# Issuing both steps of every weight split to the scheduler as if 400 instructions sooner

## The chip, the cores and the metric

The kernel runs on one core of one Trainium2 chip. The metric is device time in microseconds (us) of one execution, the median of several. Engines are named as in the profile: PE is TensorE's matmul, PEld its weight load, DVE is VectorE, ACT is ScalarE, POOL is GpSimd, SP is SyncE, which here issues DMAs only.

## The reference

Two blocks follow each other on one sequence of 512 tokens of width 1024; the first also reads 256 context tokens. Everything is float32.

```python
def first_block(x, c, ctx, ...):          # 2 hybrid layers
    ...
def hybrid_layer(xs, cs, c, c_ctx, ..., need_ctx):
    ...
    px = split_cols(hx @ w_in + b_in)     # 1024 -> N_IN
    pc = split_cols(hc @ w_in + b_in)
    ya_x = conv_module(*px[0:3], ...)     # depthwise conv of width 31, layer norm, w_conv_out
    yb_x, yb_c = gla_branch(px[3:9], pc[3:9], ...)    # 4 heads, chunks of 64, two directions
    yc_x, yc_c = attn_branch(px[9:13], pc[9:13], ...) # 8 heads, 2 key heads
    def merge(p, ya, yb, yc):
        return (jax.nn.sigmoid(p[13]) * ya + jax.nn.sigmoid(p[14]) * yb
                + jax.nn.sigmoid(p[15]) * yc) @ w_out
```

The second block has two layers, each with a big input projection, a chunked mLSTM branch and a chunked retention branch of four heads each, and an output projection.

## The kernel before, in words

**Weights.** All big weights are packed on the host into granules of 128 partitions by up to 1024 floats, in the order of use. For each granule `split` does three things: SP loads it into a tile `wr` (`raw`, L270); ACT writes its rounded high part `wh` (a copy, L285); DVE subtracts to get the low part `wl` (L286). `wr`, `wh` and `wl` have two buffers each, so a third split waits until the matmuls that read the first have ended. Some splits of block 2 and of the output projections go to spare columns of the tiles `hh` and `hl` in place of `wh` and `wl`. There are 358 splits. One small weight, that of the GLA's low-rank gate, is split by code of its own (L908, L909).

**Matmuls.** `mm3` (L317) multiplies in three passes: high by high, high by low, low by high. Activations are split into `hh`/`hl` (or `bh`/`bl` for a branch's output) in the same way. The results go to PSUM tiles called `pp`; there are three of them in block 1 and four in block 2. The matmuls that write `pp` are the projections, and PE's bulk of work.

**Order.** The program is written as one instruction sequence and a scheduler deals it out to the engines. Each engine works its list in that order. An instruction's place in the program is its priority; `tc.high_priority(offset=n)` gives the instructions inside it the priority of a place n instructions sooner. The scheduler puts what is ready, by its own reckoning, and first in priority on an engine's list first. In block 1 `_weave` writes a dependent chain (the GLA's heads, the attention's heads) and projection work by turns. `_lifted(..., 200)` already lifts the projection work that is woven into the attention, by 200; that woven into the GLA is not lifted.

**The GLA chain.** For each of four heads: a gate (`z` matmul L948, Exp and Ln on ACT, an add L953, two scans L956 and L958 on DVE, exponentials on ACT, the products `kin` L977 and `bk` L978 on DVE), transposes of `bk` on PE (L984), state products on PE (L998) and a state recurrence `SP` on DVE (L1008), masked scores (L1021, L1025), outputs on PE (L1029, L1033), then the head's norm (per-token sums L625, a reciprocal root on DVE L302 to L308, a transposing matmul L635). `bk` (L935, L936) is copied out of a `pp` tile by ACT beforehand. Last in a layer's first half the attention runs, whose value matmuls are L1264, and its output `ao` is made on DVE (L1272).

The projection work beside the chain ("fill" below) are the L317 matmuls into `pp`, whose results ACT and DVE read out (`merged` L763 and L775, `tf`).

Of the kernel before, what the change touches and what calls it, by code (L numbers as in the profile page):

```python
# [9 lines left out]
F32 = mybir.dt.float32  # L10
# [4 lines left out]
AF = mybir.ActivationFunctionType  # L15
ALU = mybir.AluOpType
# [243 lines left out]
class _K:  # L260
# [12 lines left out]
    def split(self, spec, spare=None):  # L273

        nk, nc_ = spec[3], spec[5]
        n = nk * nc_
        r = self.raw(spec)[:, :n]
        if spare is None:
            hi = self.wh.tile([P, 1024], F32R, tag="wh", name="wh")[:, :n]
            lo = self.wh.tile([P, 1024], F32R, tag="wl", name="wl")[:, :n]  # L280
        else:
            c = slice(TX + P * spare, TX + P * spare + n // KT)
            hi, lo = self.hh[:, :, c], self.hl[:, :, c]
            r = r.rearrange("p (k c) -> p k c", k=KT)
        self.nc.scalar.activation(hi, r, AF.Copy)  # L285
        self.nc.vector.tensor_tensor(out=lo, in0=r, in1=hi.bitcast(F32), op=ALU.subtract)  # L286
        return hi, lo

    @staticmethod
# [1066 lines left out]
def _second_block(K, ctx, res, pend):  # L1356
# [79 lines left out]
    for l in range(DEPTH):  # L1436
# [123 lines left out]
        def mixer(kind, hd):  # L1560
# [4 lines left out]
            if ml:  # L1565
                for which, c0 in enumerate((cq, ck)):
                    for i in range(2):
                        cc = 8 * which + 2 * hd + i
                        ps = tin(c0 + 256 * hd + 128 * i)
                        u = hp.tile([P, 515], F32, name="u", bufs=2)  # L1570
                        G.memset(u[:, 0:3], 0.0)
                        S.activation(u[:, 3:515], ps, AF.Copy)  # L1572
                        ac = tt()
                        V.tensor_scalar(out=ac, in0=u[:, 0:512], scalar1=vec("cw", 4 * cc), scalar2=vec("cb", cc),
                                        op0=ALU.mult, op1=ALU.add)
                        for t in range(1, 4):
                            V.scalar_tensor_tensor(out=ac, in0=u[:, t:t + 512], scalar=vec("cw", 4 * cc + t), in1=ac,
                                                   op0=ALU.mult, op1=ALU.add)
                        th = tt()
                        S.activation(th, ac, AF.Tanh, scale=0.5)  # L1580
                        V.scalar_tensor_tensor(out=ac, in0=th, scalar=1.0, in1=ac, op0=ALU.add, op1=ALU.mult)
                        qk.append(split(ac, 0.5 if which == 0 else 0.5 / 16, f"qk{which}{i}"))
            else:
                for which, c0 in enumerate((cq, ck)):
                    p2 = [tin(c0 + 256 * hd + 128 * i) for i in range(2)]
                    t = [tt(), tt(), tt(), tt()]
                    V.tensor_tensor(out=t[0], in0=p2[0], in1=cos, op=ALU.mult)
                    V.tensor_tensor(out=t[1], in0=p2[0], in1=sin, op=ALU.mult)
                    V.tensor_tensor(out=t[2], in0=p2[1], in1=sin, op=ALU.mult)
                    V.tensor_tensor(out=t[3], in0=p2[1], in1=cos, op=ALU.mult)  # L1590
                    V.tensor_tensor(out=t[0], in0=t[0], in1=t[2], op=ALU.subtract)
                    V.tensor_tensor(out=t[1], in0=t[1], in1=t[3], op=ALU.add)
                    for i in range(2):
                        qk.append(split(t[i], 1.0 if which == 0 else 1.0 / 16, f"qk{which}{i}"))
# [211 lines left out]
```

## Time and profile before

| | before |
|---|---|
| time, median of 3 executions | 2748.11 us (2747.8 to 2751.84) |
| profiled execution | 2749.59 us |
| span of that execution, first to last instruction | 2747.5 us |
| mean granted clock of PE | 0.977 |
| PE busy | 2609.0 us (95%) |
| DVE busy | 1984.6 us (72%) |
| ACT busy | 1089.8 us (40%) |

The span is the time in which instructions ran; some 2 us of the execution lie around it. A granted clock of 1.00 is 2.4 GHz, a stretch with 0.50 would be at 1.2 GHz all through, and a value between is a mixture of the two levels.

### The profile page before, as it was taken

What the parts mean: (1) busy time and instruction counts of PE and PEld (TensorE: products, weight loads), DVE (VectorE), ACT (ScalarE), POOL (GpSimd) and SP (SyncE); (2) the same over time, 40 slices, a digit from 0 to 9 for tenths busy, and PEclk for the clock granted to TensorE, in tenths of its full rate; (3) what the DMA queues carried; (4) which work ended last, traced back from release to release, by engine and by line L of the source; (5) the groups of instructions that cost most, each with busy time, mean ns of one, the idle gap of its engine ahead of it and who ended that gap; (6) DMA issues with size and microseconds to landing.
All of it is one profiled execution on the core that took longest, in us unless ns stands there. A gap on an engine that the chain in (4) does not pass through costs nothing.

```text
span 2747.5 us, 37004 instructions
## 1 busy us (share of the span) xinstructions
PE 2609.0 (95%) x14484; PEld 2222.0 (81%) x14484; DVE 1984.6 (72%) x3691; ACT 1089.8 (40%) x1819; POOL 27.8 (1%) x94
## 2 busy tenths in 40 slices
PE   5998899999899999699999989999999999999998
PEld 3887778888788788578877878888888978888887
DVE  5998565677875599766888678776677678655665
ACT  3234423454532334534545344442333444432332
POOL 0000000000000000000000000000000000000000
PEclk9999999999999999899999999999999999999999
DMA  5210103101253231013134424334332222223222
GB/s 210 64 56 29 39 28 103 55 30 62 71 156 100 88 97 62 27 61 112 58 111 130 139 80 137 121 117 130 123 123 77 82 82 83 84 80 92 77 85 77
DMA packets 78110, 243.18 MB, mean 89 GB/s; under 512 B 9968, under 2 KB 16496, under 8 KB 77808
## 3 DMA queue, kind: packets, MB, share of 16 engines
q1 hardware_dynamic: 72448, 233.37, 27.2%
q10 hardware_dynamic: 5488, 7.44, 0.9%
q8 instruction: 114, 1.87, 0.3%
q14 instruction: 60, 0.49, 0.1%
HBM read 238.68 MB, written 2.10 MB: 88 GB/s over the span
## 4 chain that ended last, share of the span: by engine, by line
PE 79%; DVE 15%; ACT 3%; issue 2%; DMA 1%; ACTq 0%; POOL 0%; DVEq 0%
PE pp L317 63%; PE pm L317 5%; DVE ca L814 4%; PE ov L1264 2%; DVE wl L286 2%; PE sc L1234 2%; DVE SP L1008 2%; PE tr L1254 2%; ACT wh L285 1%; PE pm L1033 1%; PE pm L635 1%; PE pm L625 1%; DVE t L958 1%; PE pm L1685 1%; DVE t L956 0%
## 5 line engine op out<-in xcount | busy, mean ns | idle before, releaser
L317 PE MATMUL pp<-hh,wh 128*128 128x512 f32 (+1 forms) x2080 | 772.5, 373 | 35.1 <-ACT bk L936 12.4
L317 PE MATMUL pp<-hh,wl 128*128 128x512 f32 (+1 forms) x2080 | 768.0, 372 | 28.8 <-DVE wl L286 28.7
L317 PE MATMUL pp<-hl,wh 128*128 128x512 f32 (+1 forms) x2080 | 767.9, 371 | 1.4 <-DVE hl L472 1.3
L285 ACT ACTIVATE wh<-wr 128x1024 fp32r<-128x1024 f32 (+1 forms) x348 | 347.6, 1000 | 769.1 <-PE pp L317 696.8
L286 DVE TENSOR_TENSOR wl<-wr,wh 128x1024 fp32r<-128x1024 f32 (+1 forms) x348 | 399.2, 1148 | 195.5 <-ACT wh L285 190.4
L317 PEld LDWEIGHTS pp<-hh,wh 128*128 128x128 f32 x2080 | 396.6, 191 | 103.2 <-ACT bk L936 13.1
L317 PEld LDWEIGHTS pp<-hh,wl 128*128 128x128 f32 x2080 | 396.4, 191 | 100.7 <-DVE wl L286 36.4
L317 PEld LDWEIGHTS pp<-hl,wh 128*128 128x128 f32 x2080 | 396.9, 191 | 64.8 <-DVE hl L472 3.4
L317 PE MATMUL pp<-wl,hh 128*128 128x256 f32 (+1 forms) x704 | 227.8, 324 | 3.4 <-DVE wl L286 3.2
L317 PE MATMUL pp<-wh,hh 128*128 128x256 f32 (+1 forms) x704 | 225.1, 323 | 3.2 <-ACT u L1572 2.7
L317 PE MATMUL pp<-wh,hl 128*128 128x256 f32 (+1 forms) x704 | 226.3, 322 | 0.0
L814 DVE SCALAR_TENSOR_TENSOR ca<-u,sm,ca 128x783 f32<-128x783 f32 (+1 forms) x240 | 201.7, 890 | 1.1
L317 PEld LDWEIGHTS pp<-wl,hh 128*128 128x128 f32 x704 | 133.8, 190 | 17.0 <-DVE wl L286 7.0
L317 PEld LDWEIGHTS pp<-wh,hh 128*128 128x128 f32 x704 | 133.2, 190 | 15.6 <-ACT u L1572 3.5
L317 PEld LDWEIGHTS pp<-wh,hl 128*128 128x128 f32 x704 | 133.8, 190 | 10.1
L417 DVE CUSTOM_DVE_ANT_0 junk<-mw,cond,bmod 128x1024 bf16<-128x1024 f32 x104 | 132.8, 1277 | 3.4 <-DMA mw<-modw 3.1
L317 PE MATMUL pp<-bh,wh 128*128 128x512 f32 (+1 forms) x288 | 105.6, 368 | 7.2 <-DVE merged L775 3.0
L317 PE MATMUL pp<-bl,wh 128*128 128x512 f32 (+1 forms) x288 | 103.4, 360 | 0.0
L317 PE MATMUL pp<-bh,wl 128*128 128x512 f32 (+1 forms) x288 | 103.2, 361 | 0.0
L317 PE MATMUL pp<-yh,wh 128*128 128x512 f32 (+1 forms) x256 | 93.9, 368 | 0.0
L317 PE MATMUL pp<-yh,wl 128*128 128x512 f32 (+1 forms) x256 | 93.5, 366 | 0.0
L317 PE MATMUL pp<-yl,wh 128*128 128x512 f32 (+1 forms) x256 | 93.4, 366 | 0.0
(377 smaller groups left out, 4266.6 us busy)
## 6 DMA issues: line engine op xcount, KB each, us to landing
wr<-wpack SPq DMA_DIRECT2D x308, 512.0 KB, 3.5
mw<-modw SPq DMA_DIRECT2D x80, 512.0 KB, 3.6
wr<-wpack SPq DMA_DIRECT2D x48, 256.0 KB, 2.7
m<-wpack SPq DMA_DIRECT2D x16, 512.0 KB, 8.2
cond<-cond ACTq DMA_DIRECT2D x5, 512.0 KB, 4.0
res<-xT SPq DMA_DIRECT2D x4, 512.0 KB, 4.9
tf<-xT SPq DMA_DIRECT2D x8, 256.0 KB, 2.6
out<-t SPq DMA_DIRECT2D x16, 128.0 KB, 1.8
```

The costliest lines, as they stand in the source:

```text
L285: self.nc.scalar.activation(hi, r, AF.Copy)
L286: self.nc.vector.tensor_tensor(out=lo, in0=r, in1=hi.bitcast(F32), op=ALU.subtract)
L317: mm(o, lhsT=lhs[a], rhs=r[b], start=first and p == 0, stop=last and p == 2)
L417: pin(V.tensor_tensor_reduce(out=junk, in0=w, in1=self.cond[:, v, :], scale=1.0, scalar=bias[:, j:j + 1], op0=ALU.mult, op1=ALU.add, accum ...
L625: T.matmul(p1[:, i:i + 1], lhsT=x[:, o:o + P], rhs=ones[:, 0:1], start=True, stop=True)
L635: T.matmul(p2[:, o:o + P], lhsT=r[:, i:i + 1].to_broadcast([P, P]), rhs=ident, start=True, stop=True)
L814: V.scalar_tensor_tensor(out=ca[:, c, :], in0=x, scalar=w, in1=ca[:, c, :], op0=ALU.mult, op1=ALU.add)
L958: V.tensor_tensor_scan(out=cum[64:128, ::-1], data0=reset[64:128, ::-1], data1=ls[64:128, ::-1], initial=0.0, op0=ALU.mult, op1=ALU.add)
L1008: V.scalar_tensor_tensor(out=SP[r, n_, :], in0=SP[r, c_, :], scalar=dec[r, c_:c_ + 1], in1=con[c_][r, :], op0=ALU.mult, op1=ALU.add)
L1234: T.matmul(sc[:, s - k0:e - k0], lhsT=qT[:, t * P:t * P + P], rhs=kT[pi][:, s:e], start=pi == 0, stop=pi == 1)
L1254: T.transpose(tr[:, jj * 256 + q * P:jj * 256 + q * P + P], pr[q][:, (j + jj) * P:(j + jj + 1) * P], ident)
L1264: T.matmul(ov, lhsT=vhl[:, kts[j0 + jj], g].rearrange("p a b -> p (a b)"), rhs=x_[:, jj * 256:jj * 256 + 256], start=j0 + jj + pi == 0, st ...
```

## The change

Both instructions of `split` are written inside `high_priority(offset=400)`. The load of `wr` and the matmuls that read `wh` and `wl` are not. Instructions, tiles, sizes and buffers are those of before.

```diff
             c = slice(TX + P * spare, TX + P * spare + n // KT)
             hi, lo = self.hh[:, :, c], self.hl[:, :, c]
             r = r.rearrange("p (k c) -> p k c", k=KT)
-        self.nc.scalar.activation(hi, r, AF.Copy)
-        self.nc.vector.tensor_tensor(out=lo, in0=r, in1=hi.bitcast(F32), op=ALU.subtract)
+        with self.tc.high_priority(offset=400):
+            self.nc.scalar.activation(hi, r, AF.Copy)
+            self.nc.vector.tensor_tensor(out=lo, in0=r, in1=hi.bitcast(F32), op=ALU.subtract)
         return hi, lo
```

The lines after it move down by one: what was L286 is L287, L317 is L318, L984 is L985. Over the whole program 76 of the 358 splits stand earlier among ACT's other work (by 1 to 23 places) and 282 stand where they stood; on DVE 149 stand earlier (by 1 to 74 places), 207 where they stood and two later by one. Their order among each other is the same. On PE more than 1125 of 13958 instructions stand elsewhere, all as a consequence; on SP 11 of 498.

**DVE's list in the GLA of layer 1**, the gate of one head, of before. `t3_9779` is the head's scanned gate, `at0`/`at1` are the scores of the head before, `bk_9200` is what PE transposes next:

```order
L1021 COPY_PREDICATED at1_8531<-masks_8511,pm_9826 128x512
L967 TENSOR_TENSOR t3_9787<-last_9782,t3_9779 128x768
L972 SCALAR_TENSOR_TENSOR bq_9128<-bq_9128,t3_9790 128x512
L1025 TENSOR_TENSOR t3_9837<-at0_8530,at1_8531 128x512
L286 TENSOR_TENSOR wl_10165<-wr_10162,wh_10164 128x1024
L977 TENSOR_TENSOR kin_9840<-bk_9200,t3_9779 128x512
L286 TENSOR_TENSOR wl_10246<-wr_10243,wh_10245 128x512
L978 TENSOR_TENSOR bk_9200<-bk_9200,t3_9787 128x768
```

The same place after. `wl_10165` and `wl_10246` now stand 24 and 17 rows further up, ahead of the scans:

```order
L287 TENSOR_TENSOR wl_10282<-wr_10279,wh_10281 128x1024
L964 COPY last_9782<-t3_9779 64x12
L1022 COPY_PREDICATED at1_8531<-masks_8511,pm_9826 128x512
L968 TENSOR_TENSOR t3_9787<-last_9782,t3_9779 128x768
L973 SCALAR_TENSOR_TENSOR bq_9128<-bq_9128,t3_9790 128x512
L1026 TENSOR_TENSOR t3_9837<-at0_8530,at1_8531 128x512
L287 TENSOR_TENSOR wl_10349<-wr_10346,wh_10348 128x512
L978 TENSOR_TENSOR kin_9840<-bk_9200,t3_9779 128x512
L776 SCALAR_TENSOR_TENSOR merged_8601<-merged_8601,pp_10249 128x512
L979 TENSOR_TENSOR bk_9200<-bk_9200,t3_9787 128x768
```

What moved: the two splits that stood just ahead of `bk` are long done there, and the next two (`wl_10282`, `wl_10349`), which stood some 40 rows behind, and a read-out of `pp` stand ahead of `bk` in their place.

**PE's list at the same place**, of before. `pp_10168` and `pp_10249` are the fill, `pm_9844` the transposes of `bk_9200`:

```order
L317 MATMUL pp_10168<-hh_8358,wh_10164 128x512
L317 MATMUL pp_10168<-hl_8359,wh_10164 128x512
L317 MATMUL pp_10249<-bh_9698,wh_10245 128x512
L317 MATMUL pp_10249<-bl_9723,wh_10245 128x512
L317 MATMUL pp_10168<-hh_8358,wl_10165 128x512
L317 MATMUL pp_10168<-hh_8358,wh_10164 128x512
L317 MATMUL pp_10168<-hl_8359,wh_10164 128x512
L317 MATMUL pp_10168<-hh_8358,wl_10165 128x512
L984 MATMUL pm_9844<-identr_58,bk_9200 128x128 x2
```

After:

```order
L318 MATMUL pp_10285<-hh_8358,wh_10281 128x512
L318 MATMUL pp_10285<-hl_8359,wh_10281 128x512
L318 MATMUL pp_10285<-hh_8358,wl_10282 128x512
...
L985 MATMUL pm_9844<-identr_58,bk_9200 128x128 x2
```

What moved: 51 matmuls of 128x512 that stood behind the transposes stand ahead of them: the last 18 of `pp_10168`, the last 10 of `pp_10249`, and 23 of `pp_10285`. At the transposes of the next head (`pm_10213`) 95 of 128x512 do so.

**PE's list where the last head of that GLA ends**, of before; `pm_10729` is the last transposing matmul of the norm:

```order
L317 MATMUL pp_10743<-bl_9723,wh_10739 128x512
L317 MATMUL pp_10743<-bh_9698,wl_10740 128x512
L635 MATMUL pm_10729<-identr_58,y_10697 128x128 x4
L317 MATMUL pp_10743<-bh_9698,wh_10739 128x512
L317 MATMUL pp_10743<-bl_9723,wh_10739 128x512
L317 MATMUL pp_10743<-bh_9698,wl_10740 128x512
L317 MATMUL pp_10792<-wh_10782,hh_8358 128x256
```

After:

```order
L318 MATMUL pp_10905<-wl_10783,hh_8358 128x256
L318 MATMUL pp_10905<-wh_10782,hl_8359 128x256
L318 MATMUL pp_10905<-wh_10782,hh_8358 128x256
L636 MATMUL pm_10729<-identr_58,y_10697 128x128 x4
L318 MATMUL pp_10905<-wl_10783,hh_8358 128x256
```

What moved: three matmuls of 128x512 (`pp_10743`) and 103 of 128x256 (48 of `pp_10792`, 48 of `pp_10846`, 7 of `pp_10905`) stand ahead of `pm_10729` and stood behind it. At the last value matmuls of layer 0's attention (`ov_6657`) 35 of 128x512 and 24 of 128x256 do so (`pp_6866`, `pp_6867`, `pp_6933`), and three splits that stood beside the last `ao` on DVE stand up to 64 rows further up. At the first transposes of layer 0's GLA (`pm_2069`) it is 20 of 128x512, and at the end of that GLA five.

## Rows read from the trace of the kernel before

**Rows 1.** The page, busy time of each engine

```profile
span 2747.5 us, 37004 instructions
...
PE 2609.0 (95%) x14484; PEld 2222.0 (81%) x14484; DVE 1984.6 (72%) x3691; ACT 1089.8 (40%) x1819; POOL 27.8 (1%) x94
```

**Rows 2.** Waits of PE, whole span (us in all, times, longest)

```profile
PE pp L317 <- DVE wl L286: 31.9, 19, 9.7
...
PE pp L317 <- ACT bk L936: 12.4, 2, 7.3
PE pp L317 <- ACT wh L285: 10.2, 7, 4.3
```

**Rows 3.** Windows: start:end, length, busy PE PEld DVE ACT POOL, granted clock, DMA

```profile
1740.00:2200.00 460.00, 458.92 (x2353) 390.01 (x2352) 320.34 (x614) 166.02 (x269) 5.94 (x16) 1.00 0.36 111
261.50:282.00 20.50, 8.09 (x32) 7.17 (x32) 19.09 (x30) 11.86 (x17) 0.00 (x0) 0.67 0.11 29
735.00:752.00 17.00, 10.92 (x70) 8.91 (x69) 15.84 (x31) 8.27 (x17) 0.00 (x0) 0.83 0.29 87
752.00:760.00 8.00, 8.00 (x30) 6.50 (x30) 5.79 (x8) 1.56 (x3) 0.00 (x0) 0.71 0.72 224
1118.50:1130.70 12.20, 1.33 (x5) 0.46 (x3) 11.76 (x21) 4.63 (x7) 0.00 (x0) 0.64 0.00 0
1130.70:1137.40 6.70, 6.63 (x34) 5.73 (x35) 2.08 (x4) 0.98 (x2) 0.00 (x0) 0.64 0.40 120
1153.70:1163.40 9.70, 0.00 (x0) 0.00 (x0) 9.54 (x13) 2.10 (x4) 0.00 (x0) 0.62 0.00 0
1163.40:1173.50 10.10, 10.09 (x44) 9.33 (x44) 1.43 (x2) 1.58 (x3) 0.00 (x0) 0.52 0.25 79
1224.00:1229.20 5.20, 5.07 (x25) 5.07 (x25) 1.28 (x3) 0.00 (x0) 0.00 (x0) 0.52 0.59 203
```

**Rows 4.** PE timeline, layer-1 GLA: start, length, instruction, idle before

```profile
1130.77 0.80 PE L317 MATMUL pp<-hh,wl 128*128 128x512 f32 x1 [8.91 <-DVE wl L286]
...
1163.41 0.79 PE L317 MATMUL pp<-hh,wl 128*128 128x512 f32 x1 [9.72 <-DVE wl L286]
```

**Rows 5.** DVE timeline of the same stretch

```profile
1129.49 1.22 DVE L286 TENSOR_TENSOR wl<-wr,wh 128x1024 fp32r<-128x1024 f32 x1
...
1131.23 0.69 DVE L286 TENSOR_TENSOR wl<-wr,wh 128x512 fp32r<-128x512 f32 x1
...
1139.41 0.16 DVE L641 TENSOR_SCALAR v<-pm 128x4 f32<-128x4 f32 x1 [6.63 <-PE pm L625]
```

**Rows 6.** Chain that ended last, 1050 to 1260: start, length

```profile
1236.18 18.66 PE pp L317 x149
```

**Rows 7.** Chain that ended last, whole span, its longest piece

```profile
2435.64 88.34 PE pp L317 x384
```

**Rows 8.** ACT timeline, layer-0 GLA

```profile
272.06 1.06 ACT L285 ACTIVATE wh<-wr 128x1024 fp32r<-128x1024 f32 x1 [5.37 <-PE pp L317]
...
277.53 0.47 ACT L935 ACTIVATE bk<-pp,sm 64x256 f32<-64x256 f32 x1
...
278.97 0.47 ACT L936 ACTIVATE bk<-pp,sm 64x256 f32<-64x256 f32 x1
```

**Rows 9.** Waits of PE from 1330 to 1520, layer-1 attention

```profile
PE pp L317 <- DVE wl L286: 3.5, 4, 2.0
PE pp L317 <- ACT wh L285: 2.8, 3, 1.5
```

**Rows 10.** Waits of PE from 735 to 752, layer-0 attention

```profile
PE pp L317 <- DVE wl L286: 1.7, 1, 1.7
```

**Rows 11.** PE timeline, the first projection

```profile
35.35 0.80 PE L317 MATMUL pp<-hh,wh 128*128 128x512 f32 x1 [4.26 <-ACT wh L285]
```

**Rows 12.** Waits of ACT, whole span

```profile
ACT wh L285 <- PE pp L317: 696.8, 243, 14.5
```

**Rows 13.** Waits of DVE, whole span

```profile
DVE wl L286 <- ACT wh L285: 190.4, 121, 8.1
```

## The prediction

> **What bounds the kernel now.** I read the page first. PE is busy 2609.0 of 2747.5 us, DVE 1984.6, ACT 1089.8 [rows 1]: PE bounds the kernel, and a change of order can only give back PE's idle time or the time in which its clock was low. Next the windows, to see where those lie. In block 2 there is nothing to win: between 1740 and 2200 us PE is busy 458.92 of 460 us at a clock of 1.00. Block 1 has holes: the start of layer 0's GLA (261.5 to 282: PE 8.09 of 20.5, DVE 19.09), the end of layer 0's attention (735 to 752: PE 10.92 of 17, DVE 15.84), and two holes of 10 to 12 us in layer 1's GLA, in which PE does 1.33 of 12.2 and 0.00 of 9.7 us while DVE is busy 11.76 and 9.54 [rows 3]. In the holes DVE is the bound: it works off a dependent chain and PE has nothing to do.
>
> Then the waits say whether PE's list was empty or only stuck. Both big holes of the GLA end at a projection matmul that needs a split's low part: 8.91 us at 1130.77 and 9.72 us at 1163.41, both released by `wl` [rows 4]. DVE's timeline shows why: that `wl` was put behind the gate's scans and scores, at 1129.49, and takes only 1.22 us; the next comes at 1131.23 with 0.69 us [rows 5]. So PE had fill, and its weights were not split. In the whole span PE waits 31.9 us for `wl` and 10.2 for `wh` [rows 2]; of the latter 4.26 us are the very first projection [rows 11], where the weight has just landed. That is all that an earlier split can remove directly. Behind a hole the clock is low as well: 0.64 from 1130.7 to 1137.4, 0.52 from 1163.4 to 1173.5 and 0.52 from 1224.0 to 1229.2 [rows 3]. Last the chain that ended last: after the GLA of layer 1 stands one piece of 149 projection matmuls, 18.66 us [rows 6]. That is fill which was left over when the dependent chain was through. Fill done earlier, inside the holes, shortens this piece; fill that can't be brought forward is worth nothing wherever the split stands.
>
> **The change part by part.** No instruction is added or removed, so the price is in the order alone.
>
> *Layer 1's GLA.* The order shows 3 matmuls of 128x512 and 103 of 128x256 moved from behind the last transposing matmul of the norm to ahead of it. A matmul of 128x512 takes 0.23 us (88.34 us for 384, [rows 7]), one of the piece after the GLA 0.125 (18.66 / 149). So 3 x 0.23 + 103 x 0.125 = 13.6 us of PE's work leave the end of this stage. They fit into the holes, which are 10.9 and 9.7 us [rows 3]. This is a gain in full if the chain on DVE ends no later. What comes on to that chain: per head two splits (1.22 + 0.69) and a read-out of 0.69 as long as the second split, 2.6 us, put ahead of `bk`; but two splits of the same sizes leave that place for one further up, where DVE also works for the chain. DVE's total stays, so a split moved by one head costs the chain about one split once, not four times. What comes off: PE at the full clock would need 6.63 x 0.64, 10.09 x 0.52 and 5.07 x 0.52 us in the three slow stretches [rows 3], that is 2.4, 4.8 and 2.4 us less. Some of these 9.6 us lie under the chain. I let the two cancel and take -13.6. Bounds: both waits go and the clock comes back, 18.6 + 9.6 = -28.2; half of the moved fill is eaten by a later chain, -6.8.
>
> *The end of layer 0's attention.* Ahead of the last value matmul come 35 matmuls of 128x512 and 24 of 128x256, 35 x 0.23 + 24 x 0.125 = 11.1 us, more than the idle time there, 17 - 10.92 = 6.1 us [rows 3]. Three splits leave the place where DVE is busy 15.84 of 17 us, and only 1.7 us of the idle time is put to `wl` by name [rows 10]. I take -5.5, nearly all of the idle time. Bounds: nothing, if the `ao` chain comes as much later as fill came forward; -8.4, with the clock of 0.71 from 752 to 760 (8.0 x 0.29 = 2.3) given back.
>
> *Layer 0's GLA.* PE waits 12.4 us, twice, for `bk`, which ACT copies out [rows 2]. At the second ACT writes `wh` at 272.06, after a wait of 5.37 for PE, and then does the gate; the four copies of `bk` come at 277.53 to 278.97 [rows 8]. After the change they stand right behind that `wh` and ahead of the gate's exponentials, some 4.3 us sooner. The order has 20 matmuls of 128x512 (4.6 us) moved ahead of the first transposes, but only five (1.1 us) at the end of this GLA. I take -3, between -1.1 and -4.6.
>
> *Layer 1's attention.* Seven waits for a split, 3.5 + 2.8 = 6.3 us [rows 9]. The splits stand 5 to 26 places sooner on DVE there. I take -4, between 0 and -6.3.
>
> *The scattered rest.* Of 31.9 + 10.2 us, 18.6 + 6.3 + 1.7 + 4.3 are spoken for; 11.2 us are left [rows 2, 4, 9, 10, 11]. Most of them stand where a split was held by something else than the order, so I take -3, between 0 and -11.
>
> *What it costs.* A lifted split stands ahead of work that PE may wait for. ACT waits 696.8 us in 243 pieces, 2.87 us each and 14.5 the longest, in front of `wh` for the matmuls that free its buffer [rows 12], and DVE 190.4 us in front of `wl` for `wh` [rows 13]. Both engines work their list in order, so whatever stands behind a waiting split waits too. Before, that was mostly idle time. I take one such stall on a path that counts, 2.9 us, and 2 us for some 50 places of block 2 where a split moved ahead of one to five other DVE instructions (two splits of 1.22 us that PE comes to wait for; PE has 1.08 us of idle time in the 460 us shown). Together +5, between 0 and what the third rival makes of it.
>
> The sum: -13.6 - 5.5 - 3 - 4 - 3 + 5 = -24.1 us. Against the profiled execution of 2749.6 us that is 2725.5; the median shown, 2748.1, lies 1.5 below it. I say 2725, a gain of 0.9%. A measurement of this kernel can tell about 0.2%, 5.5 us, from no change.
>
> **The rivals.**
>
> *More than that.* All waits for a split but the first go (31.9 + 10.2 - 4.3 = 37.8) and the slow clock behind the holes with them (9.6 + 2.3): -49.7, about 2700. For it: in the GLA of layer 1 up to 95 matmuls of 128x512, over 20 us, now stand ahead of a head's transposes. Against it: the GLA's fill ends with 13.6 us moved, not more.
>
> *The splits can't come sooner, or the waits only change their name.* 282 of 358 splits keep their place on ACT and 207 on DVE, since the two buffers of `wh` and `wl` are what holds them; ACT's 696.8 us in front of `wh` [rows 12] say so. If the scheduler's reckoning of when a buffer comes free is too early, a split stands sooner on the list and runs no sooner. Then the stages of block 1 keep their holes and the time is 2744 to 2754.
>
> *Slower: a waiting split holds up the chain.* In the GLA's holes DVE has no slack (11.76 of 12.20, [rows 3]). Each head's `bk` now stands behind two further splits and a read-out, 2.6 us, and each of these can wait: for the matmuls of the fill through `wh`, 2.87 us on average [rows 12]. At 5.5 us for each of four heads of layer 1, and 2.9 us for each of four of layer 0, the chain is 33.5 us later, less 13.6 of fill and some 4 in the attention: +16, about 2766. It decides from 13.6 / 4 = 3.4 us of lateness per head of layer 1 on. Against it: the fill that frees the buffers now runs sooner too, in the holes, so the splits behind it should find their buffer free.
>
> The Trainium skill (Perfetto Trace Analysis, section "Tensor Engine Instruction (MATMUL, LD_WEIGHTS)") states that ACT and DVE queues are strictly first in, first out, while PE alone may pull a weight load ahead of matmuls. By that rule every blocked split blocks its engine, which is this rival's mechanism; the trace agrees as far as it goes, with DVE's `wl` never passed by the instruction listed behind it [rows 5].
>
> **How the numbers follow.** A gain of 10 to 40 us: 0.57. More than that: 0.13. Within 0.2% (2743 to 2753): 0.13. Slower: 0.17. So faster 0.70, same 0.13, slower 0.17. The range from 2703 to 2756 leaves out about half of the biggest gain and most of the losses; the forecast's own goes from 2709 to 2739.
>
> **What would show it.** Right: the piece of 149 projection matmuls after layer 1's GLA falls to about 43; PE's waits for `wl` fall from 31.9 to some 10 us; the stretch from 1118 to 1174 has PE busy in it and a higher clock; `bk` in layer 0 follows its `wh` at once. Wrong: PE waits for `bk` (L979), `merged` or `ao` grow by as much as those for `wl` fall; DVE's wait in front of `wl`, or ACT's in front of `wh`, lies in the GLA's gate, between the scans and `bk`; block 2 gets idle time on PE at evacuations.

## The result, and the profile after

The changed kernel takes 2728.26 us (median of 4 runs, 2723.83 to 2733.16), the kernel before in the same sessions 2749.47 us (2747.8 to 2751.84). The ratio is 0.9918, 95% interval 0.9905 to 0.993: 0.8% faster. The forecast was 2725 us, a gain of 24.1 us on the profiled execution; the medians differ by 21.2 us, the spans of the two profiled executions by 2747.5 - 2728.5 = 19.0 us. Of these 19.0 us, 16.0 are idle time of PE (138.5 us before, 122.5 after) and 3.0 its busy time (2609.0 and 2606.0).

PE's waits over the whole span, after (line waited for: us in all, times, longest):

```profile
PE pp L318 <- DVE wl L287: 9.7, 9, 3.2
PE pp L318 <- ACT bk L937: 9.0, 3, 4.0
PE pp L318 <- DVE merged L776: 8.6, 1, 8.6
PE pp L318 <- ACT wh L286: 7.9, 5, 4.3
PE pp L915 <- DVE wh L910: 7.6, 1, 7.6
PE pp L318 <- ACT tf L741: 5.7, 2, 4.8
```

Against [rows 2] the wait for `wl` falls from 31.9 to 9.7 us, for `bk` from 12.4 to 9.0, for `wh` from 10.2 to 7.9. Five waits are new or longer: 8.6 us in one piece for a read-out `merged` (5.0 in three pieces before), 7.6 for the small low-rank weight, whose split the change doesn't lift (4.7 before), 5.7 for the read-out `tf` in layer 0's attention (2.5 before), 3.9 for `bh` of the attention's output, and 3.0 for a gate's `t` in layer 0's GLA. 28 us of waits went and not all of that was kept.

The windows show the two holes of layer 1's GLA mostly filled (start:end, length, busy PE, PEld, DVE, ACT, POOL, granted clock, DMA):

```profile
258.00:279.00 21.00, 12.32 (x51) 10.67 (x52) 20.22 (x35) 14.42 (x22) 0.00 (x0) 0.63 0.07 26
725.00:760.00 35.00, 30.19 (x183) 26.13 (x183) 32.88 (x58) 16.73 (x34) 0.00 (x0) 0.95 0.31 89
1106.00:1170.00 64.00, 58.03 (x323) 47.70 (x323) 49.48 (x105) 33.22 (x50) 0.00 (x0) 0.97 0.17 53
1170.00:1200.00 30.00, 21.38 (x121) 18.41 (x119) 23.37 (x43) 12.37 (x18) 0.00 (x0) 0.81 0.24 73
```

The third line spans the two holes of [rows 3], 1118.5 to 1130.7 and 1153.7 to 1163.4. PE is busy 58.03 of 64 us there, the granted clock is 0.97, where stretches of 0.52 and 0.64 stood before. At the start of layer 0's GLA (first line) the clock is still low, 0.63. And a hole has come in further on: in the 30 us of the last line PE is busy 21.38 us at a clock of 0.81, and the wait of 8.6 us for `merged` lies there. Over the whole stage, from the low-rank matmul to the end of the fill left over, before and after:

```profile
1013.78:1254.84 241.06, 212.04 (x1291) 179.99 (x1289) 188.18 (x355) 103.01 (x149) 0.00 (x0) 0.92 0.18 58
1002.60:1234.07 231.47, 211.28 (x1290) 183.49 (x1289) 186.48 (x354) 99.59 (x146) 0.00 (x0) 0.94 0.19 58
```

PE's idle time falls from 29.0 to 20.2 us and its busy time from 212.0 to 211.3: what this stage wins is idle time, and next to nothing comes from the clock.

The chain that ended last, after, from 1040 to 1260, one piece:

```profile
1229.14 4.93 PE pp L318 x41
```

It answers to [rows 6]: of the fill left over behind the GLA 41 matmuls remain where there were 149, and 4.93 us where there were 18.66. That is 13.7 us, the 13.6 of the prediction. But the piece begins at 1229.14 where it began at 1236.18, 7.0 us sooner, and this GLA's first matmul (the low-rank one, L914, now L915) begins 11.2 us sooner. So the chain itself has become longer by 4.1 us. These rows of the two lines give the length of the chain, from that first matmul to the start of the last transposing matmul of the norm:

```profile
L915 PE MATMUL pp<-hh,wh x16: 276/334/398, 1002.6 to 1007.9; 128*64 128x512 f32 x8, 128*64 128x256 f32 x8
...
L636 PE MATMUL pm<-identr,y x40: 274/276/506, 1092.7 to 1228.9; 128*128 128x128 f32 x40
```

1228.9 - 1002.6 = 226.3 us after; before, the same two rows give 1235.9 - 1013.8 = 222.1.

Read at the same instruction in both traces, the change gave by stage:

| from, to (before) | predicted | measured |
|---|---|---|
| start to layer 0's low-rank matmul, 158.8 | 0 | +1.7 |
| to the attention's first transposes, 470.1 (layer 0's convolution and GLA) | -3 | -7.2 |
| to layer 1's low-rank matmul, 1013.8 (layer 0's attention and output) | -5.5 | -5.7 |
| to the last matmul of the fill left over, 1254.8 (layer 1's GLA) | -13.6 | -9.6 |
| to block 2's first gate transposes, 1637.9 (layer 1's attention and output) | -4 | +1.0 |
| to the end, 2747.5 | +2 | +0.8 |
| scattered waits, a stall on the path | -3, +3 | in the rows above |
| sum | -24.1 | -19.0 |

The whole is near, three of the stages are not: both GLAs and layer 1's attention. The +1.7 of the first row can't be told from chance: in the change and in eight of the kernels below, which have one and the same order on PE, ACT and DVE up to that matmul, it starts between 157.9 and 162.3 us. In the later stages kernels with one order agree within about 2 us.

**Why the chain is longer.** DVE's timeline, after, the gate of the head that the order showed (start, length, instruction):

```profile
1117.69 1.75 DVE L959 TENSOR_TENSOR_SCAN t<-reset,t 64x768 f32<-64x768 bf16 x1
...
1120.29 1.21 DVE L287 TENSOR_TENSOR wl<-wr,wh 128x1024 fp32r<-128x1024 f32 x1
...
1123.82 0.69 DVE L1026 TENSOR_TENSOR t<-at,at 128x512 f32<-128x512 f32 x1
1124.42 0.70 DVE L287 TENSOR_TENSOR wl<-wr,wh 128x512 fp32r<-128x512 f32 x1
1125.03 0.69 DVE L978 TENSOR_TENSOR kin<-bk,t 128x512 f32<-128x512 f32 x1
1125.63 0.69 DVE L776 SCALAR_TENSOR_TENSOR merged<-merged,pp 128x512 f32<-128x512 f32 x1
1126.23 0.96 DVE L979 TENSOR_TENSOR bk<-bk,t 128x768 f32<-128x768 f32 x1
```

The same two instructions before:

```profile
1123.86 1.75 DVE L958 TENSOR_TENSOR_SCAN t<-reset,t 64x768 f32<-64x768 bf16 x1
...
1131.83 0.96 DVE L978 TENSOR_TENSOR bk<-bk,t 128x768 f32<-128x768 f32 x1
```

From the end of the second scan to the start of `bk` it takes 1126.23 - (1117.69 + 1.75) = 6.8 us after and 1131.83 - (1123.86 + 1.75) = 6.2 us before. So here DVE costs the chain 0.6 us, not 2.6: two splits and a read-out entered, two splits left, as the prediction said. DVE isn't idle there and no split waits for its buffer. The lateness is there before this: counted from the stage's first matmul the scan starts at 1117.69 - 1002.6 = 115.1 us after and at 1123.86 - 1013.8 = 110.1 us before, 5.0 us apart. ACT's timeline, after, a little sooner:

```profile
1087.07 0.69 ACT L937 ACTIVATE bk<-pp,sm 64x512 f32<-64x512 f32 x1
1087.77 0.68 ACT L936 ACTIVATE bk<-pp,sm 64x512 f32<-64x512 f32 x1
1088.47 1.06 ACT L286 ACTIVATE wh<-wr 128x1024 fp32r<-128x1024 f32 x1
1089.56 0.47 ACT L936 ACTIVATE bk<-pp,sm 64x256 f32<-64x256 f32 x1
1090.04 1.16 ACT L937 ACTIVATE bk<-pp,sm 64x256 f32<-64x256 f32 x2
1091.22 0.47 ACT L936 ACTIVATE bk<-pp,sm 64x256 f32<-64x256 f32 x1
```

Before, the `wh` at this place stood behind all four copies of 64x512:

```profile
1098.84 0.68 ACT L936 ACTIVATE bk<-pp,sm 64x512 f32<-64x512 f32 x1
1100.59 1.06 ACT L285 ACTIVATE wh<-wr 128x1024 fp32r<-128x1024 f32 x1 [1.07 <-issue]
```

PE and DVE after, at the same place:

```profile
1091.25 0.50 PE L318 MATMUL pp<-hh,wh 128*128 128x512 f32 x1 [2.00 <-ACT bk L937]
...
1092.70 2.00 PE L636 MATMUL pm<-identr,y 128*128 128x128 f32 x8
```

```profile
1090.17 1.22 DVE L287 TENSOR_TENSOR wl<-wr,wh 128x1024 fp32r<-128x1024 f32 x1
1091.31 0.15 DVE L309 SCALAR_TENSOR_TENSOR y<-t,g 128x4 f32<-128x4 f32 x1
...
1092.49 0.16 DVE L309 SCALAR_TENSOR_TENSOR y<-t,y 128x4 f32<-128x4 f32 x1
```

The lifted copy of 1.06 us now stands ahead of the last copy of 64x512 that empties a `pp` tile, and PE waits 2.00 us for the tile; behind five such matmuls stand on PE's list the transposes of the convolution's norm and the GLA's state products. The Trainium skill (Perfetto Trace Analysis, section "Tensor Engine Instruction (MATMUL, LD_WEIGHTS)") says that ACT's queue is strictly first in, first out; the rows agree, since no copy of `bk` passes the `wh` ahead of it. That wait alone isn't the delay, though: the transposes also need `y`, which is ready only at 1092.49 + 0.16 = 1092.65, because a subtract of 1.22 us, whose `wh` had just been written, has got in between the steps of the norm's root. Counted from the stage's first matmul, `y` is 2.2 us later than before. Behind PE's wait the granted clock is 0.76 (1091 to 1098; before, from 1101.8 to 1108.2, 1.00), and the eight transposes take 2.00 us where they took 1.14. A second split gets into the rest of the convolution's part (ACT 1103.07, DVE 1104.16). So copy and subtract both stand in the chain here. The experiments take the two steps apart.

**Where layer 1's attention's gain went.** PE's waits from 1315 to 1585, after:

```profile
PE pp L318 <- DVE t L470: 5.7, 1, 5.7
PE pp L318 <- ACT bh L746: 3.9, 1, 3.9
PE pp L318 <- ACT wh L286: 0.8, 1, 0.8
...
PE pp L318 <- DVE wl L287: 0.3, 1, 0.3
```

The splits' waits fell from 6.9 us (6.3 in the shorter stretch of [rows 9]) to 1.1 us, as forecast. In their place stands one of 3.9 us for the attention's output: PE reached the matmuls that need `bh` before the output was there. The 5.7 us for the norm stood there before as 5.8 us (for `hh`, L471). Over the whole stage of the table PE's idle time falls by only 1.5 us (16.9 to 15.4), and its busy time rises by 2.5 us (366.2 to 368.7) at a granted clock of 0.98 where it was 0.99. So a wait for weights became a wait for the chain, and PE's longer busy time took back more than the rest.

### The profile page after: what moved, and what is told of

It reads as the page before. It is cut to its first block, busy times and chain, and to the rows that moved or that the text cites. A ratio compares the mean times of both kernels' runs of the same rounds, so it can differ in the third digit from the quotient of the medians.

```text
span 2728.5 us, 37038 instructions
## 1 busy us (share of the span) xinstructions
PE 2606.0 (96%) x14484; PEld 2223.3 (81%) x14484; DVE 1986.8 (73%) x3691; ACT 1090.1 (40%) x1819; POOL 27.5 (1%) x94
## 3 DMA queue, kind: packets, MB, share of 16 engines
q1 hardware_dynamic: 72448, 233.37, 27.7%
## 4 chain that ended last, share of the span: by engine, by line
PE 52%; DVE 4%; ACT 1%; issue 1%; DMA 0%; POOL 0%; DVEq 0%; ACTq 0%
PE pp L318 43%; PE pm L318 5%; PE ov L1265 1%; PE sc L1235 1%; DVE wl L287 1%; PE tr L1255 1%; DVE SP L1009 1%; PE pm L1686 1%; ACT wh L286 0%; PE pm L1034 0%; PE pm L1030 0%; PE pm L999 0%; DVE t L1421 0%; PE pm L636 0%; DMA wr<-wpack 0%
## 5 line engine op out<-in xcount | busy, mean ns | idle before, releaser
L318 PE MATMUL pp<-hh,wh 128*128 128x512 f32 (+1 forms) x2080 | 773.5, 374 | 32.7 <-ACT bk L937 9.0
L318 PE MATMUL pp<-hh,wl 128*128 128x512 f32 (+1 forms) x2080 | 769.7, 372 | 7.0 <-DVE wl L287 6.8
L318 PE MATMUL pp<-hl,wh 128*128 128x512 f32 (+1 forms) x2080 | 768.5, 371 | 1.4 <-DVE hl L473 1.1
L286 ACT ACTIVATE wh<-wr 128x1024 fp32r<-128x1024 f32 (+1 forms) x348 | 347.8, 1000 | 739.2 <-PE pp L318 670.3
L287 DVE TENSOR_TENSOR wl<-wr,wh 128x1024 fp32r<-128x1024 f32 (+1 forms) x348 | 399.3, 1148 | 191.5 <-ACT wh L286 184.4
L318 PEld LDWEIGHTS pp<-hh,wh 128*128 128x128 f32 x2080 | 397.7, 192 | 100.2 <-ACT hh L472 10.5
L318 PEld LDWEIGHTS pp<-hh,wl 128*128 128x128 f32 x2080 | 397.4, 191 | 75.2 <-DVE wl L287 10.7
L318 PEld LDWEIGHTS pp<-hl,wh 128*128 128x128 f32 x2080 | 398.0, 192 | 64.3 <-DVE hl L473 3.3
L318 PE MATMUL pp<-wh,hh 128*128 128x256 f32 (+1 forms) x704 | 227.1, 326 | 12.3 <-DVE merged L776 8.6
L318 PE MATMUL pp<-wl,hh 128*128 128x256 f32 (+1 forms) x704 | 229.5, 326 | 3.1 <-DVE wl L287 2.9
L318 PE MATMUL pp<-wh,hl 128*128 128x256 f32 (+1 forms) x704 | 228.0, 324 | 0.0
L318 PEld LDWEIGHTS pp<-wh,hh 128*128 128x128 f32 x704 | 134.6, 192 | 24.4 <-issue 9.5
L318 PEld LDWEIGHTS pp<-wl,hh 128*128 128x128 f32 x704 | 135.2, 192 | 16.8 <-DVE wl L287 6.7
L318 PEld LDWEIGHTS pp<-wh,hl 128*128 128x128 f32 x704 | 135.1, 192 | 10.0
L318 PE MATMUL pp<-bh,wh 128*128 128x512 f32 (+1 forms) x288 | 105.6, 369 | 4.0 <-ACT bh L746 3.9
L318 PE MATMUL pp<-bl,wh 128*128 128x512 f32 (+1 forms) x288 | 103.6, 362 | 0.0
L318 PE MATMUL pp<-bh,wl 128*128 128x512 f32 (+1 forms) x288 | 103.0, 361 | 0.0
L318 PE MATMUL pp<-yh,wh 128*128 128x512 f32 (+1 forms) x256 | 94.0, 368 | 0.0
L318 PE MATMUL pp<-yh,wl 128*128 128x512 f32 (+1 forms) x256 | 93.5, 366 | 0.0
L318 PE MATMUL pp<-yl,wh 128*128 128x512 f32 (+1 forms) x256 | 93.5, 366 | 0.0
```

What stands on the lines that cost most here:

```text
L318: mm(o, lhsT=lhs[a], rhs=r[b], start=first and p == 0, stop=last and p == 2)
```

## The experiments

Twelve kernels ran, each timed against the kernel before on the same chip (2750.1 to 2751.8 us). "Left" is the number of projection matmuls, and their time, in the piece behind layer 1's GLA, where the chain that ended last shows it as one piece; "chain" is the length of that GLA as above. There is one trace of each kernel. How far one chain length can be trusted: e2 and e12, with one order on PE, ACT and DVE in this stage, have 221.4 and 220.8 us; the change and e9, whose orders there differ in two matmuls of PE alone, have 226.3 and 228.5.

| run | lifted | time, us | ratio (95%) | left | chain, us | PE for `wl`, us |
|---|---|---|---|---|---|---|
| before | - | 2749.5 | 1 | 149, 18.66 | 222.1 | 31.9 |
| the change | both, 400 | 2728.3 | 0.9918 (0.9905 to 0.993) | 41, 4.93 | 226.3 | 9.7 |
| e1 | copy only, 400 | 2738.7 | 0.9954 (0.994 to 0.9968) | 143, 17.61 | 225.7 | 27.4 |
| e2 | subtract only, 400 | 2718.8 | 0.9884 (0.9869 to 0.9898) | - | 221.4 | 9.5 |
| e3 | both, GLA parts | 2723.2 | 0.9893 (0.9878 to 0.9907) | 42, 5.04 | 224.3 | 14.1 |
| e4 | both, rest of block 1 | 2746.4 | 0.9984 (0.9975 to 0.9992) | 143, 17.61 | 220.6 | 26.3 |
| e5 | both, 100 | 2722.6 | 0.99 (0.9886 to 0.9913) | 107, 13.28 | 223.4 | 23.9 |
| e6 | both, 200 | 2733.7 | 0.9938 (0.9925 to 0.995) | 82, 10.28 | 221.6 | 17.7 |
| e7 | both, and gates 450 | 2734.1 | 0.9943 (0.9931 to 0.9956) | 46, 5.52 | 224.5 | 6.2 |
| e8 | both, and read-outs 400 | 2729.5 | 0.9925 (0.9911 to 0.9938) | - | 225.3 | 13.6 |
| e9 | subtract; copy in GLA parts | 2721.3 | 0.9883 (0.9867 to 0.9899) | - | 228.5 | 10.9 |
| e10 | subtract; copy elsewhere | 2721.8 | 0.9896 (0.9882 to 0.9909) | 40, 4.80 | 217.4 | 8.7 |
| e11 | subtract only, 100 | 2733.3 | 0.9935 (0.9923 to 0.9948) | 107, 13.30 | 222.9 | 24.9 |
| e12 | subtract only, GLA parts | 2724.6 | 0.9906 (0.9893 to 0.992) | 49, 5.89 | 220.8 | 11.7 |

### One step alone

```diff
-        with self.tc.high_priority(offset=400):
-            self.nc.scalar.activation(hi, r, AF.Copy)
-            self.nc.vector.tensor_tensor(out=lo, in0=r, ...)
+        self.nc.scalar.activation(hi, r, AF.Copy)        # e2
+        with self.tc.high_priority(offset=400):
+            self.nc.vector.tensor_tensor(out=lo, in0=r, ...)
```

e1 has it the other way round, with the copy inside. Expected of e1:

> Only ACT's copy (the high part) is issued 400 sooner; DVE's subtract stays. Theory: what counts in layer 1's GLA is DVE's place for the low part. The order shows 141 projection matmuls of 128x256 left behind the last head of that GLA (147 before, 41 with both steps lifted), so nothing is won there, and PE's waits of 8.9 and 9.7 us for the low part stay; only the copies of bk in layer 0's GLA come sooner, some 4 us. Time about 2745 against 2749.5 before. Rival (the copy is the step that was late, since ACT waits 697 us in front of it): about 2730, as with both.

Expected of e2:

> Only DVE's subtract (the low part) is issued 400 sooner; ACT's copy stays. Theory: 49 matmuls of 128x256 left behind the last head of layer 1's GLA, so almost all of the gain there (9 us) and at the end of layer 0's attention (5 us); the 7 us of layer 0's GLA, where ACT's list decides when bk is copied, mostly not. Time about 2734. Rival (a subtract can't come before its copy, so lifting it alone does little): about 2745.

e2 is the best kernel of the study, 32.2 us below its kernel before (2750.91) and better than the change, with intervals that don't overlap. It was expected at 2734; both its theory and its rival were too high. PE's waits in e2:

```profile
PE pp L318 <- DVE wl L287: 9.5, 11, 1.8
PE pp L318 <- ACT bk L937: 8.9, 2, 6.1
PE pp L318 <- DVE merged L776: 8.9, 1, 8.9
```

The wait for `wl` is as short as with both steps. In e1 it stays,

```profile
PE pp L318 <- DVE wl L287: 27.4, 15, 9.7
```

with the longest of 9.7 us unchanged and the leftover piece at 143 matmuls. So the subtract's place alone fills the holes of layer 1's GLA: this part of the theory holds. What e1 wins lies by its trace in layer 0's attention and output (-9.0) and in layer 1's attention (-1.9), not in layer 0's GLA, where -4 was expected and 0.1 lost; in layer 1's GLA it loses 2.5. Of the four copies of `bk` behind the late `wh` in layer 0's GLA, e1 has two behind it and two still among the gate's exponentials. And in e2 layer 0's GLA gives -10.5, the copies of `bk` standing directly behind their `wh` as with both. So the forecast's reason for the gain in layer 0's GLA, a lifted copy that draws those of `bk` forward, falls: lifting the subtract does it.

### One part of the program alone

The offset is a variable that is 0 except while the named part is written. Expected of e3 (convolution and GLA parts):

> Both steps lifted by 400, but only while the convolution and GLA part of each layer of block 1 is written. By the two traces (the same instruction in both) the change loses 1.8 us up to 200 us, wins 7.3 in layer 0's GLA, 4.5 in layer 0's attention and what follows, 9.2 in layer 1's GLA up to the attention's first projections, nothing in layer 1's attention, and loses 1 in block 2. Theory (the stages add up): 2749.5 + 1.8 - 7.3 - 9.2 = about 2735. Rival (the attention's gain is owed to the state in which the GLA leaves the queues, so that the stages do not add): about 2729.

Expected of e4 (the rest of block 1):

> Both steps lifted by 400, but only from the attention of each layer of block 1 to the layer's end. Theory (stages add up): -4.5 in layer 0, nothing in layer 1, about 2745. 141 matmuls stay behind the last head of layer 1's GLA. Rival (the stages do not add): no change, 2749.

e4 came out as its theory said. e3 is 27.7 us below its kernel before, not 14, nearer its rival. By stages e3 gives -4.9 from 158.8 to 470.1, -8.1 in layer 0's attention and output, where none of its splits is lifted, and -11.5 in layer 1's GLA. The stages don't add: lifting a split in the GLA changes where everything behind it stands, also in parts that aren't lifted. By their traces, of PE's 2070 instructions from the end of the leftover piece to block 2's first gate e3 has some 450 in another place than before.

### Smaller offsets

```diff
-        with self.tc.high_priority(offset=400):
+        with self.tc.high_priority(offset=100):          # e5; 200 in e6
```

> Offset 100 in place of 400. The order leaves 105 matmuls of 128x256 behind the last head of layer 1's GLA (147 with none, 41 with 400): 5.6 us of fill moved there in place of 13.6, and the chain about 2 us late in place of 5.9. Theory (the gain goes with the fill moved, less what the splits hold up): about 2742. Rival (a small lift gets the splits past the fill without getting them into the chain, so it is as good or better): 2725 to 2730.

> Offset 200. 80 matmuls left behind the last head of layer 1's GLA, 8.7 us of fill moved. Theory: between, about 2736. Rival as with offset 100: 2725 to 2730.

The leftover piece falls with the offset, as the order said (147, 105, 80, 41 of 128x256): 149, 107, 82, 41 matmuls for 0, 100, 200, 400. In e5 the chain that ended last has

```profile
1219.84 13.28 PE pp L318 x107
```

The times don't follow it: 2749.5, 2722.6, 2733.7, 2728.3. e6 is near its theory, and e5 is better than even its rival said. In layer 1's GLA up to the end of that piece e5 wins 4.1 us (1254.84 - 1233.12, less the 17.6 that it had won by 1013.8), somewhat under the 5.6 us of fill moved; its other gains are -12.2 in layer 0's attention and output and some 6 in layer 1's attention. PE still waits 23.9 us for `wl` in e5, more than twice as long as with the change, which is slower. The theory holds for the stage and fails for the whole, since the attention stages vary by as much as the GLA gives.

Part of that variation can be put to two waits of PE. In layer 0's attention and output a wait of 3.6 to 4.8 us for `tf` (L741 of the change) stands in six kernels (the change, e4, e6, e7, e8, e10), and the stage takes 536.8 to 540.1 us; in six others (e1, e2, e3, e5, e9, e11) it takes 531.4 to 535.9; before and in e12, where PE still waits 2.1 us for `ao` at the attention's end, 543.6 and 543.8. In layer 1's attention the wait of 3.9 us for `bh` stands in the change, e2, e4, e6, e7, e10 and e11, whose stage takes 382.8 to 385.1 us, and not in e1, e3, e5, e9 and e12, with 377.2 to 381.3 (before, with its waits for splits, 383.1; e8, which has the wait, isn't comparable, since more of its work lies behind the boundary). With both steps lifted, offset 100 has neither wait at that length, 200 and 400 have both. Which place on which list brings them about wasn't found.

### What holds the chain and the fill

Expected of e7, in which the gates of heads 1 to 3 are lifted by 450:

```diff
-    ahead = ... else gla_gate(hd + 1) if hd < 3 else iter(())
+    ahead = ... else _lifted(tc, gla_gate(hd + 1), 450) if hd < 3 else iter(())
```

> The change, and the gates of the GLA's heads 1 to 3 (up to the transposes of bk) lifted by 450, so that they stand ahead of the lifted splits. 46 matmuls left behind the last head of layer 1's GLA, so nearly as much fill is moved (12.9 us). Theory: the chain of layer 1's GLA ends 5.9 us later with the change because two splits and a read-out stand ahead of each bk; with the gates lifted the 5.9 us come back in good part, about 2723. Rival (the chain is late because PE's list now has more fill ahead of each of its matmuls, not because of DVE's splits): same as the change, 2728, or slower, since the fill's splits come late again.

Of PE's waits in e7 one has grown (2.2 us with the change, 3.3 before):

```profile
PE pm L985 <- DVE bk L979: 13.1, 5, 6.0
...
PE pp L318 <- DVE wl L287: 6.2, 8, 1.7
```

The gate's transposes were lifted too, on PE's list, past the fill; PE stands in front of them 13.1 us until DVE has `bk`. Head 1's `bk` does come 8.1 us sooner than with the change, counted from the stage's first matmul (115.5 against 123.6 us), but the chain is 224.5 us, only 1.8 shorter, and the time 2734.1. The expected 2723 fails, and the rival's "same or slower" is met in the number. Neither reading is settled by it, since the edit made a wait of its own.

Expected of e8:

```diff
+                    with tc.high_priority(offset=400):
                         V.scalar_tensor_tensor(out=th[:, s:e], in0=th[:, s:e], scalar=1.0, in1=ps, ...)
```

> The change, and the read-out of the merge's second projection on DVE (the multiply into the gate's tile) lifted by 400 too. With the change PE has one new wait of 8.6 us for such a read-out (merged) in layer 1's GLA, which had gone to the fill's low part before. With it lifted the order leaves no matmul behind the last head of that GLA, so 18.7 us of fill are moved in place of 13.6. Theory (the fill is now held by its PSUM tiles): 5 us more, less up to 2.8 us by which four read-outs of 0.69 us hold the chain up: about 2725. Rival (the chain is what bounds this stage, and each piece of work put ahead of it costs in full): 2733 or more.

It answers to this row of PE's timeline of the change, with the fill stuck behind the last read-out ahead of `bk`:

```profile
1192.89 0.55 PE L318 MATMUL pp<-wh,hh 128*128 128x256 f32 x1 [8.62 <-DVE merged L776]
```

e8 is at 0.9925, the change at 0.9918: no difference that the intervals show. Neither the 2725 of the theory nor the 2733 of its rival came. The wait for `merged` is gone from the list of long ones and that for `wl` is 13.6 us in place of 9.7: in part the wait changed its name. The GLA's fill is out at 1223.7 us, ahead of the end of the chain, but the attention's first transposes start at 1253.9 us where the change has 1252.8: the chain is hardly shorter (225.3 us), and with no fill left behind it nothing more is won there.

### Where the lifted copy costs

Expected of e9, subtract lifted everywhere and copy only in the GLA parts:

> DVE's subtract lifted by 400 everywhere, ACT's copy only while the convolution and GLA parts are written. DVE's step alone gave 2718.8, both 2728.3. Theory (a lifted copy that waits for its buffer, or merely takes its 1.06 us, stands ahead of the copies of bk and the gate's steps on ACT, and the GLA's chain with it): the loss lies in the GLA parts, so this kernel is at about 2727. Rival (the loss lies in the attention, where the trace of the change shows the same instruction 7.6 us later than at the GLA's end): about 2719.

Expected of e10, the complement:

> The complement: DVE's subtract lifted by 400 everywhere, ACT's copy everywhere but in the convolution and GLA parts. Theory (the loss of lifting the copy lies in the GLA): about 2720. Rival (it lies in the attention): about 2727.

The chain's length separates them. First and last rows of layer 1's GLA in e2:

```profile
L915 PE MATMUL pp<-hh,wh x16: 276/334/398, 996.1 to 1001.4; 128*64 128x512 f32 x8, 128*64 128x256 f32 x8
...
L636 PE MATMUL pm<-identr,y x40: 275/275/376, 1083.6 to 1217.5; 128*128 128x128 f32 x40
```

in e9:

```profile
L917 PE MATMUL pp<-hh,wh x16: 276/334/398, 998.0 to 1003.3; 128*64 128x512 f32 x8, 128*64 128x256 f32 x8
...
L638 PE MATMUL pm<-identr,y x40: 275/276/422, 1088.7 to 1226.5; 128*128 128x128 f32 x40
```

and in e10:

```profile
L917 PE MATMUL pp<-hh,wh x16: 276/334/398, 1000.4 to 1005.7; 128*64 128x512 f32 x8, 128*64 128x256 f32 x8
...
L638 PE MATMUL pm<-identr,y x40: 274/276/377, 1088.0 to 1217.8; 128*128 128x128 f32 x40
```

These are 221.4, 228.5 and 217.4 us. Over all runs at an offset of 400 the chain takes 224.3 to 228.5 us in the six kernels with the copy lifted in the GLA (the change, e1, e3, e7, e8, e9), and 217.4 to 221.4 in the four without (e2, e4, e10, e12). Three pairs differ only in whether the copy is lifted in the GLA parts: the change and e10 (8.9 us longer with the lift), e9 and e2 (7.1), e3 and e12 (3.5). So lifting the copy makes the chain of layer 1's GLA longer, by 3.5 to 8.9 us, and lifting the subtract alone doesn't. How, the rows of e2 say at the place shown above for the change: without the lift the copy is done at 1083.82, and the subtract, lifted as it is, stands behind the last step of the norm's root in place of in it:

```profile
1083.40 0.16 DVE L309 SCALAR_TENSOR_TENSOR y<-t,y 128x4 f32<-128x4 f32 x1
1083.85 1.22 DVE L287 TENSOR_TENSOR wl<-wr,wh 128x1024 fp32r<-128x1024 f32 x1 [0.29 <-ACT wh L285]
```

It is the early copy that lets the lifted subtract into the chain there. In e1, with the copy alone lifted, ACT's list at this place is that of before, and its chain of 225.7 us gets longer further on; that wasn't followed up. Layer 0's GLA shows the same loss: 304.1, 306.5 and 306.0 us in the change, e3 and e9, and 302.9, 301.4 and 300.9 in e10, e12 and e2.

In the whole time it is less plain: e9 has the longer chain and gets 0.9883, the same as e2 within the intervals; e10 0.9896. The copy lifted in either part costs nothing that can be measured, lifted in both it costs some 10 us. What e9 loses to e2 in the two GLAs, 11.2 us, it has back but for 2.4 us in the two attention stages (3.4 and 5.4 us); it has no wait for `bh`, and e2 has. Neither theory nor rival said that.

### The subtract alone, less of it

> DVE's subtract alone, lifted by 100. 105 matmuls of 128x256 stay behind the last head of layer 1's GLA, 49 with the subtract lifted by 400. Theory (the gain of DVE's step goes with the fill it brings forward): 56 x 0.125 = 7 us less of it, about 2726. Rival (a short lift keeps the subtract out of the chain, which with both steps gave 2722.6 at 100 and 2733.7 at 200): 2719 or better.

> DVE's subtract alone, lifted by 400, in the convolution and GLA parts only. With it lifted everywhere the stages gave, against before: -11.7 up to the end of layer 0's GLA, -6 in layer 0's attention and after, -13.2 in layer 1's GLA, -1.5 in layer 1's attention. Theory (the GLA carries the gain; what the attention gives is a by-product of where the GLA leaves the lists): about 2722 to 2726. Rival (the attention's own lift brings 6 to 8 us): 2727 to 2731.

e12 is where its theory put it. e11 is slower than both its expectations; the leftover piece has 107 matmuls, as in e5, and e5 with the copy lifted as well is some 10 us faster. An offset of 100 is good with both steps (e5) and poor with one (e11), while 400 is better with one. By their traces e5 and e11 part in the attention stages, by 3.7 us in layer 0 and 7.3 in layer 1, where e11 has the wait of 3.9 us for `bh` and e5 doesn't; why only one of them has it stays open. The theory of e12 is right on the GLA (-9.9 and -14.0 us in the two) and on layer 0's attention, where it wins nothing (+0.1).

## Why the prediction was right, point by point

**What bounds the kernel.** Right, and mostly by the first of the two: 16.0 us of PE's idle time were won and 3.0 us of its busy time; block 2 moved by +0.8 us against +2.

**Layer 1's GLA, -13.6.** The mechanism and the size of the moved fill are right: fill in place of holes, 41 matmuls left, 13.7 us. The step that was off is "I let the two cancel", the returned clock against the later chain. Of the 9.6 us that the clock was to give back 0.8 came (PE busy 212.04 and 211.28 us): a new hole of 8.6 us, with a clock of 0.81 around it, stands behind the two that were filled. And the chain is 4.1 us longer. So -9.6. The cause named beside it, two splits and a read-out ahead of `bk` on DVE, is small (0.6 us at the head shown). What lengthens the chain is that the copy is lifted with the subtract: 3.5 to 8.9 us in three pairs.

**The end of layer 0's attention, -5.5.** The size is right (-5.7) for the stage up to layer 1, the reason is not shown, and that the sum came out is in part luck. Half of it is idle time (-2.9) and half busy time (-2.8), where the forecast had nearly all of the idle time, and a wait of 4.8 us for `tf` came in. The stage gives -8.1 in e3 and +0.1 in e12, and in neither are its splits lifted.

**Layer 0's GLA, -3.** Mis-sized, -7.2, and for another reason than ACT's order alone: e1, with only the copy lifted, wins nothing there, e2 with only the subtract -10.5. The sign named was there, `bk` right behind its `wh`, and the second wait for `bk` did shrink, from 7.34 to 2.96 us. Of the 7.2 us, 4.7 are PE's idle time, about the forecast's bound of 4.6, and 2.5 are its busy time, at a granted clock of 0.95 where it was 0.94, a term that the forecast didn't have for this stage.

**Layer 1's attention, -4.** Wrong, +1.0. The waits for the splits went, 5.8 of 6.9 us, and a wait for the attention's output of 3.9 us took their place; the step that failed is that a wait that ends sooner is time won, where the next thing that PE needs is the chain's output. PE's busy time rose by 2.5 us besides. It is the first of the signs named for a wrong prediction, in one stage; in layer 1's GLA the same sign shows in `merged`, 1.1 us before and 8.6 after.

**What it costs, +5.** Near in size: the 4.1 us by which the chain of layer 1's GLA got longer stand for the one stall of 2.9 us, and block 2 gave +0.8 for 2. The low-rank weight's wait, 2.9 us longer, wasn't forecast. ACT waits in front of `wh` no longer than before, 670.3 us and 696.8, so in sum a lifted split waits no longer; in the rows shown its price is its own duration.

**The rivals.** Not more than that: the change's waits for splits did fall, but not to nothing, and the clock came back only in small part; e2 comes nearest with 2718.8. That the splits can't come sooner is refuted by the piece of 41; that the waits only change their name holds for a part of them (`merged`, `bh`, `tf`). That a split holds up the chain is true of its place, a copy ahead of those of `bk` and a subtract in the norm's root, but by its own duration and not by its wait, and not of its price: 4.1 us in all and not 5.5 per head, under the bound of 13.6 us from which it would have decided.

**Open.** Which places on the lists bring about the waits for `tf` and `bh`, with which the attention stages differ (+0.1 to -12.2 us in layer 0, whatever is lifted there), and with them why the copy's lift costs some 10 us in the whole only when it is lifted everywhere and why the times aren't monotone in the offset. More buffers for `wh` and `wl`, which would show whether the two buffers hold the copy, weren't tried.

## What to carry to other kernels

Raise the step that is late, not the pair: the holes waited for DVE's subtract, and lifting it alone was worth 32 us where lifting it with ACT's copy was worth 21; in each of three pairs the early copy made the GLA's chain longer. What a bulk engine gains from weights that are ready sooner is the work that leaves the end of the dependent stage; it can be counted from the two orders before a run (147, 105, 80, 41 matmuls here, and 149, 107, 82, 41 in the traces), while the waits that vanish from a list can't be added up, since the next wait takes part of them. With a scheduler that deals out by priority, a lift in one stage changes the stages behind it by as much as it wins in its own, so one such change is judged by the whole time, stage by stage with PE's idle and busy time apart, and neighbouring settings are worth a run.
